# Twelve more projections of a hybrid attention/mLSTM layer computed in the seven-product stage, and what runs between the attention heads instead

## The chip, the cores and the metric

The kernel runs on one core of one Trainium2 chip. A core has a matrix engine (TensorE, "PE" in the profile; its weight loads are "PEld"), a vector engine (VectorE, DVE), an activation engine (ScalarE, ACT), GpSimd (POOL), SyncE (SP), which issues most transfers, and 16 DMA engines. The metric is the device time of one execution in microseconds (us). Three executions of the kernel before took 1817.91, 1818.23 and 1819.29 us; the median is 1818.23 us.

## The reference

One layer of a diffusion trunk for 640 tokens (128 context, 512 latent) of 1024 channels: a half-step SwiGLU feed-forward, then attention and an mLSTM (a chunkwise recurrent matrix memory) side by side on the same normalised input, then a second feed-forward. Cut to what matters here, with `h` the normalised input (640 x 1024):

```
mq, mk, mv, mo, mg, dq, dk, dv, gm, gd = split_cols(h @ p['w_in'][l])
dq = rmsnorm(dq, p['g_qn'][l]); dk = rmsnorm(dk, p['g_kn'][l])
q_att = rope_2d(dq)                                   # latent tokens
keys = jnp.concatenate([rope_2d(dk), k_ctx], axis=1)  # and the values with v_ctx
att = diff_attention(q_att, keys, vals, lam)          # 8 heads, 2 x 64 wide

# in it, for each block of 128 queries:
s = jnp.einsum('bqhcd,bkhcd->bhcqk', qi, kf) * scale
pr = jax.nn.softmax(s, axis=-1)
w = pr[:, :, 0] - lam * pr[:, :, 1]
out = jnp.einsum('bhqk,bkhv->bqhv', w, vf)

q = heads(mq) * (ML_HEAD_DIM ** -0.5)                 # 4 heads of 256: a factor of 1/16
h_f, st_f = mlstm_chunkwise(q, k, v, ...)             # k = heads(mk), v = heads(mv); and backwards
hm = rmsnorm(h_f + rev(h_b)) * jax.nn.sigmoid(mo)
y = jax.nn.sigmoid(gm) * (hm @ p['w_br_m'][l]) + jax.nn.sigmoid(gd) * (att @ p['w_br_d'][l])
```

The change is about where and how `mq`, `mk` and `mo` are computed. Everything is in float32; a product is made of three matmuls of split halves (high by high, high by low, low by high).

## The kernel before

The core keeps `h` transposed as two tiles `hH` and `hL` (high and low half; 8 blocks of 128 channels by 640 tokens). A weight slice of 1024 x 256, a *granule*, arrives as `raw` (1 MB) and is split into `wH` (by ACT) and `wL` (by DVE).

Three ways to project a granule occur:
- a **feature unit** (`feat_unit`, PSUM tile `ps_p`, four to a granule): 128 output channels by 320 tokens, 24 matmuls that each stream 320 columns;
- a **token unit** (`tok_unit`, `ps_t`, five to a granule): 128 tokens by 256 output channels, 24 matmuls of 256 columns;
- the **seven-product stage** (class `Winograd`, here its subclass `Gates`, `ps_f`): the granule is treated as a 2 x 2 block matrix, and seven products of 12 matmuls of 320 columns take the place of the eight that four feature units are. It needs sums of weight blocks (`ww`, `wB`, `wC`, made by DVE and ACT from `raw`) and sums of the four blocks of `h` (`S`, made once). Partial results `u` are added to others on DVE to `g_out`, which SP stores to DRAM.

The program in order: first feed-forward (to about 455 us of the span); the first pair's `q` and `k` as token units; `Gates`, six granules (`w_gd` and `w_gm`, three each; about 504 to 578 us); attention (to about 1065 us); the mLSTM loop, called the memory stage below (to about 1212 us); gates, output projection and second feed-forward.

Attention is eight heads (`hd`) of five query blocks (`qi`; blocks 0 to 3 against 768 keys, block 4 against 128). The loop at L1942 writes for each block: `scores` (PE, tile `sc`, then DVE's minimum `mn`), `turn` of the block before (PE transposes the weights `p` into `ps_wT`, ACT copies them to `wT`), `soft` (two exponentials on ACT), `mix` (DVE: `rc`, `r`, then `p`), `values` of the block before (PE: `ps_o` from `wT`; DVE: `ao`). At block 3 it writes `pack` of the next head (ACT: `qpk`, twice `kpk`; DVE: `qpk`), and at the head's end `queries` and `keys` (PE transposes them, ACT and DVE copy). Blocks under `with written()` keep the written order on each engine.

Between these steps PE gets units from a queue, `Fill` (L1244): `fill.units(n)` issues the next n units of the queue in its order, filled at L1757 to L1781. The table `UNITS` says how many go to the two places of each block and to the places at the head's end. The units of the attention's own later pairs (`project_q`, `project_k`, `project_v` of pairs 1 to 3) are in the same queue; after a pair's five units `qk_norm_rope` (L1467) normalises and rotates the tokens: ACT squares (`rope`), DVE sums (`ss`), multiplies by `ry` and the weight, ACT swaps halves (`rope`), DVE multiplies with two tables and adds. I call this a *rope* below. What is left in the queue after attention is issued in the memory stage.

`Columns` (L787) computes parts of the modulation vector: DVE multiplies and sums slices `raw_a` of a weight matrix, two instructions of 128 x 1024 to a tile. The memory stage holds twelve such tiles.

ACT and DVE take their instructions one after the other in the order of the program.

Of the kernel before, what the change touches and what calls it, by code (L numbers as in the profile page):

```python
# [16 lines left out]
D = 1024  # L17
# [14 lines left out]
def tile_trunk(ctx: ExitStack, tc: tile.TileContext, a: dict):  # L32
# [287 lines left out]
    class Winograd:  # L320
# [57 lines left out]
        def copy_of(self, p, tag, bufs=1):  # L378
            t = self.tmp.tile([128, HALF], F32, tag=tag, name="u", bufs=bufs)
            self.copied = act(t, p, AF.Copy)  # L380
            return t

        def products(self, work, between, then=(), ahead=None, prepared=False, narrow=0):
# [16 lines left out]
            for i, (gr, A, done, used) in enumerate(work):  # L400
# [32 lines left out]
                u2 = copy_of(Y, "nacc" if i < 2 * FB - 2 else "nsq", 2)  # L433
# [6 lines left out]
                u3 = copy_of(Y, "nry")  # L440
# [889 lines left out]
    gd_dram = dp.tile([128, KT, T], F32, name="gd_dram")  # L1330
    qq_dram = dp.tile([128, 2, T], F32, name="qq_dram")
# [130 lines left out]
    def rope_place(of):  # L1462
        if not in_pools:
            return rope_p[0].tile([128, 5, 256], F32, tag="pk", name="rope", bufs=2)
        return pair(of, 2, "rope").rearrange("p a b -> p (a b)").rearrange("p (t n) -> p t n", t=5)
# [39 lines left out]
    def project_k(pr, now=lambda f: f()):  # L1505
        def make():
            if pr % 2:
                t = pair("k", 3, "k_tok").rearrange("p a b -> p (a b)").rearrange("p (t n) -> p t n", t=5)
            else:
                t = qk.tile([128, 5, 256], F32, tag="ktok", name="k_tok")  # L1510
# [15 lines left out]
    def project_v(pr):  # L1526
        def make():
            v_tok[pr] = t = ap.tile([128, 7, 256], F32, tag="vtok", name="v_tok")
# [163 lines left out]
    def begin_pools():  # L1692
        gates.close()
        in_pools["k"] = ctx.enter_context(tc.tile_pool(name="mlk", bufs=1, side="right"))
        in_pools["q"] = queries_of.enter_context(tc.tile_pool(name="mlq", bufs=1, side="right"))
# [21 lines left out]
    def k_evac(h, by_act=False):  # L1717
        mkT[h] = pair("k", h, "mkT")
        if by_act:
            return lambda p, mt, hf: act(mkT[h][:, mt, half(hf)], p, AF.Copy)  # L1720
        return lambda p, mt, hf: vec.tensor_copy(mkT[h][:, mt, half(hf)], p)
# [18 lines left out]
    def queries_of_memory(h):  # L1740
        feature(a["w_mq"][h], lambda: q_evac(h))

    def keys_of_memory(h, **kw):
        feature(a["w_mk"][h], lambda: k_evac(h, **kw))

    def open_gate(h, pool):
        feature(a["w_mo"][h], lambda: o_evac(h, pool()))

# [17 lines left out]
    keys_of_memory(1)  # L1766
    values_of(1)
    token(project_v(2))
    values_of(2)
    projections(3)  # L1770
    open_gate(1, attention)
    values_of(3)
    token(project_v(3))
    queries_of_memory(2)
    keys_of_memory(2)
    queries_of_memory(3)
    keys_of_memory(3, by_act=True)
    open_gate(2, memory)
    open_gate(3, memory)
# [13 lines left out]
    class Gates(Winograd):  # L1793


        def __init__(self, fp, tmp, psum):
            self.fp, self.tmp, self.psum = fp, tmp, psum
            self.part = {(kh, hf): Of(kh, hf) for kh in range(2) for hf in range(2)}
            self.work = [
                [Granule(4, lambda raw, src=src[g]: dma(raw, src)), lambda i: self.ops[i], self.done(dst, g), lambda i: None]  # L1800
                for g in range(3) for src, dst in ((a["w_gd"], gd_dram), (a["w_gm"], gm_dram))
            ]
# [4 lines left out]
        def done(self, dst, g):  # L1807
            def f(mt, hf, p, u):
                t = self.tmp.tile([128, HALF], F32, tag=("nsq", "nt")[mt], name="g_out", bufs=2)
                if u is None:  # L1810
                    act(t, p, AF.Copy)
                else:
                    tt(vec, t, p, u, ALU.add)
# [73 lines left out]
    def between(i, at):  # L1887
        if at and i < 4:
            with tc.issue_after(G.work[i + 1][0].split_at):
                (lambda: None, tables, *ropes)[i]()  # L1890
        elif (i, at) == (len(G.work) - 2, 0):
# [3 lines left out]

    G.products(G.work, between, narrow=2)
    wide.close()
    early.close()
# [18 lines left out]
    def aside(hd, qi, part):  # L1917
# [11 lines left out]
    two, one = (1, 1), (1, 0)  # L1929
    UNITS = {  # L1930
        0: (two, two, two, two, two, (1, 1, 1)), 1: (two, two, two, one, one, (1,)),
        2: (two, two, two, two, two, (1, 1, 1)), 3: (two, two, two, one, one, (1,)),
        4: (two, two, two, two, two, (1, 1, 1)), 5: (two, two, two, two, one, (1,)),
        6: (one,) * 5 + ((0, 0, 0),), 7: (one,) * 4 + ((0, 0),),
    }
    late = None
    for hd in range(8):
        H = heads[hd]
        odd = hd % 2
        for qi in range(5):  # L1940
# [20 lines left out]
            if (hd, qi) == (0, 2):  # L1961
                begin_pools()
            fill.units(n[1])
# [5 lines left out]
        if hd < 7:  # L1969
# [6 lines left out]
            if odd:  # L1976
                for i in range(5):
                    fill.one()
                    if i in (0, 1):
                        N.keys(i)  # L1980
                    if i == 1:
                        with written():
                            fill.ahead()
            else:
# [555 lines left out]
```

## Time and profile before

| | |
|---|---|
| times | 1817.91, 1818.23, 1819.29 us |
| profiled execution | span 1816.4 us; its last instruction ends there, and the fastest of the three times lies 1.5 us above it, the median 1.8 us |
| PE busy | 1793.6 us (99%) |
| DVE busy | 1323.8 us (73%) |
| ACT busy | 894.8 us (49%) |
| POOL busy | 37.1 us (2%) |
| mean DMA rate | 169 GB/s |

"Busy" is the time in which an engine has an instruction under way. The PE's instruction ends are modelled and overlap, so what a matmul costs is read from the distance between starts of neighbours, not from its listed duration. A group's row names line, engine, operation, output and inputs, shapes and count, then total and mean time; after the bar follow the engine's idle time just before these instructions and what ended it. In a timeline row the first number is the start, the second the duration, and the bracket the idle time before. The shares of busy time are means over stages that have different limits.

### The profile page before, as it was taken

How to read it: one execution, taken by the hardware profiler on the slowest of the kernel's cores; microseconds unless marked ns; L12 is line 12 of the kernel's file. 1: busy time of each engine (PE TensorE's matmuls, PEld its weight loads, DVE VectorE, ACT ScalarE, POOL GpSimd, SP SyncE). 2: the span in 40 equal slices, each digit the busy share in tenths (PEclk: the TensorE clock that was granted, in tenths of full speed). 3: DMA queues.
4: the chain of work that ended last, by engine and by line, in shares of the span. 5: the costliest groups of instructions: out<-in, count | busy, mean ns of one | idle time of the engine just before them, and what ended most of it. 6: DMA issues, size and time to landing. Idle time of an engine off the chain costs nothing.

```text
span 1816.4 us, 30813 instructions
## 1 busy us (share of the span) xinstructions
PE 1793.6 (99%) x12622; PEld 1754.8 (97%) x12622; DVE 1323.8 (73%) x2140; ACT 894.8 (49%) x1558; POOL 37.1 (2%) x65
## 2 busy tenths in 40 slices
PE   9999999999999999999999999999999999999998
PEld 7999999999999999999999889999999999999998
DVE  6889986677886776475575649876767888897485
ACT  5654553333755454455465454674336545554432
POOL 0000000100000000000000000000000000000010
PEclk9999999999999999999999999999999999999999
DMA  8255566977244322112222055665652355657992
GB/s 330 106 197 183 185 224 235 344 228 257 82 138 159 106 76 78 63 63 89 80 89 72 20 169 163 223 254 183 238 170 80 134 172 185 202 181 275 352 307 83
DMA packets 130622, 307.69 MB, mean 169 GB/s; under 512 B 9841, under 2 KB 92017, under 8 KB 117553
## 3 DMA queue, kind: packets, MB, share of 16 engines
q1 hardware_dynamic: 120114, 263.64, 42.1%
q0 software_dynamic: 9680, 39.46, 6.7%
q8 instruction: 99, 1.62, 0.4%
q10 hardware_dynamic: 688, 2.63, 0.4%
q14 instruction: 41, 0.34, 0.1%
HBM read 238.14 MB, written 67.56 MB: 168 GB/s over the span
## 4 chain that ended last, share of the span: by engine, by line
PE 84%; DVE 7%; DMA 5%; ACT 3%; issue 1%; SPq 0%; DVEq 0%; ACTq 0%
PE ps_f L75 43%; PE ps_p L75 19%; PE ps_t L75 11%; PE sc L75 3%; PE ps_o L75 2%; DVE ww L54 2%; PE ps_n L75 2%; DMA raw<-in_w2b 2%; DMA raw_a<-in_w_ada_k 1%; PE ps_wT L78 1%; PE ps_u L75 1%; DVE junk L813 1%; PE ps_qkT L78 1%; DMA out_new_c<-Cn 1%; DMA P<-nm_dram 1%
## 5 line engine op out<-in xcount | busy, mean ns | idle before, releaser
L75 PE MATMUL ps_f<-S,ww 128*128 128x320 f32 x2184 | 352.5, 310 | 3.0 <-DMA S<-g_dram 1.0
L75 PEld LDWEIGHTS ps_f<-S,ww 128*128 128x128 f32 x2184 | 327.5, 188 | 7.0 <-DVE ww L54 4.6
L75 PE MATMUL ps_p<-hH,wH 128*128 128x320 f32 x672 | 212.4, 316 | 0.7 <-DVE stage L61 0.7
L75 PE MATMUL ps_p<-hH,wL 128*128 128x320 f32 x672 | 207.7, 309 | 0.0
L75 PE MATMUL ps_p<-hL,wH 128*128 128x320 f32 x672 | 207.7, 309 | 0.0
L54 DVE TENSOR_TENSOR ww<-raw,ww 128x2048 fp32r<-128x2048 f32 (+1 forms) x67 | 150.2, 2241 | 63.7 <-ACT ww L51 63.6
L75 PE MATMUL ps_f<-hm,ww 128*128 128x320 f32 x1176 | 185.8, 309 | 0.6 <-DVE ww L54 0.6
L75 PE MATMUL ps_t<-wH,hH 128*128 128x256 f32 x640 | 185.2, 289 | 0.9 <-DVE x L57 0.9
L75 PE MATMUL ps_t<-wH,hL 128*128 128x256 f32 x640 | 181.0, 283 | 0.9 <-DVE hL L54 0.9
L75 PE MATMUL ps_t<-wL,hH 128*128 128x256 f32 x640 | 180.8, 283 | 0.0
L75 PEld LDWEIGHTS ps_f<-hm,ww 128*128 128x128 f32 x1176 | 175.7, 188 | 1.2 <-DVE ww L54 1.2
L75 PE MATMUL ps_f<-hm,wB 128*128 128x320 f32 x1008 | 161.5, 309 | 0.0
L51 ACT ACTIVATE ww<-raw 128x2048 fp32r<-128x2048 f32 (+1 forms) x67 | 125.3, 1871 | 57.9 <-DVE raw L54 33.6
L75 PEld LDWEIGHTS ps_f<-hm,wB 128*128 128x128 f32 x1008 | 151.3, 188 | 0.0
L54 DVE TENSOR_TENSOR raw<-raw 128x1024 f32<-128x1024 f32 x168 | 145.3, 865 | 1.9
L75 PEld LDWEIGHTS ps_p<-hH,wH 128*128 128x128 f32 x672 | 126.4, 188 | 1.2 <-DVE stage L61 0.9
L75 PEld LDWEIGHTS ps_p<-hL,wH 128*128 128x128 f32 x672 | 126.3, 188 | 0.3
L75 PEld LDWEIGHTS ps_p<-hH,wL 128*128 128x128 f32 x672 | 126.2, 188 | 0.0
L51 ACT ACTIVATE u<-ps_f 128x320 f32<-128x320 f32 x117 | 50.7, 433 | 153.2 <-PE ps_f L75 153.1
L75 PEld LDWEIGHTS ps_t<-wH,hH 128*128 128x128 f32 x640 | 122.3, 191 | 1.5 <-ACT nsq L51 1.1
L75 PEld LDWEIGHTS ps_t<-wH,hL 128*128 128x128 f32 x640 | 122.3, 191 | 1.1 <-DVE hL L54 1.1
L75 PEld LDWEIGHTS ps_t<-wL,hH 128*128 128x128 f32 x640 | 122.5, 191 | 0.4
(307 smaller groups left out, 3444.8 us busy)
## 6 DMA issues: line engine op xcount, KB each, us to landing
g_dram<-g SPq DMA_DIRECT2D x44, 640.0 KB, 7.5
raw_a<-in_w_ada_c POOLq DMA_DIRECT2D x31, 512.0 KB, 4.7
g_dram<-g SPq DMA_DIRECT2D x24, 480.0 KB, 8.2
raw<-in_w1b SPq DMA_DIRECT2D x11, 1024.0 KB, 4.8
raw<-in_w3b SPq DMA_DIRECT2D x11, 1024.0 KB, 6.3
raw<-in_w1a SPq DMA_DIRECT2D x10, 1024.0 KB, 4.9
raw<-in_w3a SPq DMA_DIRECT2D x10, 1024.0 KB, 6.5
hm<-g_dram SPq DMA_DIRECT2D x7, 1280.0 KB, 13.3
```

Source lines behind the costliest of these rows:

```text
L51: return placed(nc.scalar.activation(*args, **kw))
L54: return placed(eng.tensor_tensor(out=out, in0=in0, in1=in1, op=op))
L75: tc.keep_in_program_order(nc.tensor.matmul(*args, **kw))
L78: tc.keep_in_program_order(nc.tensor.transpose(*args, **kw))
L813: placed(vec.tensor_tensor_reduce(out=junk, in0=raw, in1=self.csil[:, v, :], op0=ALU.mult, op1=ALU.add, scale=1.0, scalar=0.0, accum_out=m ...
```

## The change

The twelve granules `w_mq`, `w_mk`, `w_mo` (four heads each) leave the queue and join `Gates.work`, which has 18 granules instead of six. Their results go to DRAM (`mq_dram`, `mk_dram`, `o_dram`; the first two are new); keys are loaded again during head 6 (`load_keys`), queries after attention (`load_queries`). The queue holds token units only, except for the last two granules, and its order is heads' own projections first (`k`, `q`, `v` of pairs 1, 2, 3), then the memory's values. `UNITS` is one unit to a block and three at a head's end. Eight of the memory stage's twelve `Columns` tiles move into eight of the new granules. `q_tok` and `k_tok` of odd pairs, and every second `v_tok`, get a second place.

```diff
         def products(self, work, between, then=(), ahead=None, prepared=False, narrow=0):
...
-                u2 = copy_of(Y, "nacc" if i < 2 * FB - 2 else "nsq", 2)
+                scaled = getattr(gr, "scaled", {})
+                u2 = copy_of(Y, "nacc" if i < 2 * FB - 2 else "nsq", 2, **scaled)
...
-                u3 = copy_of(Y, "nry")
+                u3 = copy_of(Y, "nry", **scaled)
...
     def rope_place(of):
...
-        return pair(of, 2, "rope")...
+        return pair("k", "qk".index(of), "rope")...
...
-            q_tok[pr] = t = qk.tile([128, 5, 256], F32, tag="qtok", name="q_tok")
+            q_tok[pr] = t = (ap if pr % 2 else qk).tile([128, 5, 256], F32, tag="qtok", name="q_tok")
...
-    def o_evac(h, pool):
-        def f(p, mt, hf):
-            t = pool.tile([128, HALF], F32, tag="stage", name="stage", bufs=2)
-            ts(t, p, -43.0, ALU.max)
-            act(t, t, AF.Exp, scale=-1.0)
-            nc.sync.dma_start(out=o_dram[:, 2 * h + mt, half(hf)], in_=t)
-        return f
...
-    def q_evac(h):
+    def load_queries(h):
         mqT[h] = pair("q", h, "mqT")
-        return lambda p, mt, hf: act(mqT[h][:, mt, half(hf)], p, AF.Copy, scale=0.0625)
+        nc.sync.dma_start(out=mqT[h], in_=mq_dram[:, 2 * h : 2 * h + 2, :])
...
     token(project_v(0))
-    open_gate(0, attention)
     values_of(0)
-    projections(1)
-    queries_of_memory(0)
-    keys_of_memory(0)
-    token(project_v(1))
-    queries_of_memory(1)
-    projections(2)
...
-    open_gate(3, memory)
+    for pr in range(1, 4):
+        projections(pr)
+        token(project_v(pr))
+    for h in range(1, 4):
+        values_of(h)
     gate_unit(a["w_gm"], gm_dram, 3, memory)
     gate_unit(a["w_gd"], gd_dram, 3, memory)
...
+            gate = [(a[n], dst, g, self.plain) for g in range(3) for n, dst in (("w_gd", gd_dram), ("w_gm", gm_dram))]
+            qk = [(a[n], dst, h, f) for h in range(4) for n, dst, f in (("w_mq", mq_dram, self.query), ("w_mk", mk_dram, self.plain))]
+            o = [(a["w_mo"], o_dram, h, self.opening) for h in range(4)]
+            self.work = []
+            for src, dst, g, f in gate[:5] + qk[:3] + o[:1] + qk[3:5] + o[1:2] + qk[5:7] + o[2:3] + qk[7:] + o[3:] + gate[5:]:
+                gr = Granule(4, lambda raw, src=src[g]: dma(raw, src))
...
+        elif (i, at) in IN_GATES:
+            columns.tile(G.at_vec)
...
+    IN_GATES = [(i, 1) for i in (5, 6, 7, 9, 10, 12, 13, 15)]
...
-    two, one = (1, 1), (1, 0)
-    UNITS = {
-        0: (two, two, two, two, two, (1, 1, 1)), 1: (two, two, two, one, one, (1,)),
-        2: (two, two, two, two, two, (1, 1, 1)), 3: (two, two, two, one, one, (1,)),
-        4: (two, two, two, two, two, (1, 1, 1)), 5: (two, two, two, two, one, (1,)),
-        6: (one,) * 5 + ((0, 0, 0),), 7: (one,) * 4 + ((0, 0),),
-    }
+    one = (1, 0)
+    UNITS = {hd: (one,) * 5 + ((1, 1, 1),) for hd in range(7)}
+    UNITS[5] = UNITS[6] = (one,) * 5 + ((1, 1, 0),)
+    UNITS[7] = (one,) * 4 + ((0, 0), (0, 0))
...
+            elif hd == 6 and qi < 4:
+                load_keys(qi)
...
-            fill.drain(5)
+            fill.drain(2)
...
+    load_queries(0)
...
-    fill.pace(1.4, 1)
+    fill.pace(0.6, 1)
...
-    columns.place(12, csil2, load_columns_raw, 1)
+    for h in range(1, 4):
+        load_queries(h)
+    columns.place(4, csil2, load_columns_raw, 1)
...
-            if n in ((3, 5, 7, 8), (1, 3, 6, 8), (1, 3, 5, 7), ())[h]:
+            if n in ((5,), (3, 7), (5,), ())[h]:
                 columns.tile(m.at_vec)
```

How this moves instructions is shown at three places. The first is DVE in head 1, from the minimum of block 3 (the reduction of its scores `sc`) to block 4's `p`. Before:

```order
L1614 TENSOR_REDUCE mn_7940<-sc_7931 128x2
L54 TENSOR_TENSOR wL_7927<-raw_7738,wH_7926 128x2048
L1628 RECIPROCAL rc_7942<-sm_7941 128x2
L57 SCALAR_TENSOR_TENSOR r_7986<-sm_7941,nlam_5309,rc_7942 128x1
L57 SCALAR_TENSOR_TENSOR p0_7955<-p1_7956,r_7986,p0_7955 128x768
L61 TENSOR_SCALAR ao_7412<-ps_o_7990,rc_7844 128x128
L54 TENSOR_TENSOR qpk_7998<-q_tok_6819,qpk_7998 128x5x128
L1614 TENSOR_REDUCE mn_8035<-sc_8030 128x2
L54 TENSOR_TENSOR kL_8150<-ck_8171,kH_8149 128x2x256
L1628 RECIPROCAL rc_8037<-sm_8036 128x2
L57 SCALAR_TENSOR_TENSOR r_8080<-sm_8036,nlam_5309,rc_8037 128x1
L57 SCALAR_TENSOR_TENSOR p0_8050<-p1_8051,r_8080,p0_8050 128x128
```

After, from block 2's `ao`, which stands right behind block 3's `p`, to block 4's minimum:

```order
L61 TENSOR_SCALAR ao_8135<-ps_o_8612,rc_8451 128x128
L54 TENSOR_TENSOR kL_8694<-ck_8715,kH_8693 128x2x256
L57 SCALAR_TENSOR_TENSOR rt_8509<-ry_8508 128x20
L54 TENSOR_TENSOR rt_8509<-rt_8509,rv_8507 128x20
L57 SCALAR_TENSOR_TENSOR ry_8508<-rt_8509,ry_8508 128x20
L54 TENSOR_TENSOR q_tok_8239<-q_tok_8239,ry_8508 128x1280
L54 TENSOR_TENSOR q_tok_8239<-q_tok_8239,g_qn_5295 128x256
L54 TENSOR_TENSOR rope_8517<-rope_8517,ropeBq_5314 128x1024
L54 TENSOR_TENSOR q_tok_8239<-q_tok_8239,ropeAq_5313 128x1024
L54 TENSOR_TENSOR q_tok_8239<-q_tok_8239,rope_8517 128x1024
L54 TENSOR_TENSOR qpk_8620<-q_tok_8239,qpk_8620 128x5x128
L1614 TENSOR_REDUCE mn_8631<-sc_8626 128x2
```

Before, the second pair's query rope was over by then, and one subtraction (`qpk`) stood between block 3's `p` and block 4's minimum. After, the rope's second half stands there, because the fifth unit of `q_tok_8239` is issued in block 2 of this head.

The second place is ACT at the same point, from the second exponential of block 3 (`p1`) on. Before:

```order
L51 ACTIVATE p1_7956,sm_7941<-sc_7931,mn_7940 128x768
L51 ACTIVATE qpk_7998<-q_tok_6819 128x5x2x64
L51 ACTIVATE kpk_8001<-k_tok_6542 128x10x64 x2
L51 ACTIVATE k_tok_7899<-ps_t_7960 128x256
L51 ACTIVATE k_tok_7899<-ps_t_8004 128x256
L51 ACTIVATE kH_8149<-ck_8171 128x2x256
L51 ACTIVATE wT_8039<-ps_wT_8040 128x512
L51 ACTIVATE wT_8039<-ps_wT_8046 128x256
L51 ACTIVATE p0_8050,sm_8036<-sc_8030,mn_8035 128x128
```

After:

```order
L51 ACTIVATE p1_8567,sm_8552<-sc_8542,mn_8551 128x768
L51 ACTIVATE v_tok_8580<-ps_t_8582 128x256
L51 ACTIVATE kH_8693<-ck_8715 128x2x256
L51 ACTIVATE rt_8509<-rv_8507 128x20
L51 ACTIVATE ry_8508<-rt_8509 128x20
L51 ACTIVATE rope_8517<-q_tok_8239 128x1024
L51 ACTIVATE v_tok_8580<-ps_t_8650 128x256
L51 ACTIVATE qpk_8620<-q_tok_8239 128x5x2x64
L51 ACTIVATE kpk_8623<-k_tok_7846 128x10x64 x2
L51 ACTIVATE wT_8635<-ps_wT_8636 128x512
L51 ACTIVATE wT_8635<-ps_wT_8642 128x256
L51 ACTIVATE p0_8646,sm_8632<-sc_8626,mn_8631 128x128
```

Before, `qpk` follows the exponentials at once, as `q_tok_6819` is ready; the copies `wT_8039` of block 3's weights come behind the packing. After, `qpk_8620` needs the rotated `q_tok_8239`, and the copies `wT_8635` of block 3's weights still stand behind it.

The third place is SP's queue where the memory stage begins (`P` is a decay matrix, `va` the values, `C` the state, `csil` the conditioning vector). Before:

```order
L97 DMA mask_11300<-in_mask 128x256
L97 DMA P_11302<-nm_dram_4640 128x5x128 x2
L97 DMA va_11303<-v_dram_4635 128x5x256
L97 DMA C_11313<-in_c_aug 128x516
L97 DMA C_11315<-in_c_aug 128x516
L97 DMA csil_11317<-csil_dram_88 128x2048
L2023 DMA P_11456<-nm_dram_4640 128x5x128 x2
L2026 DMA va_11457<-v_dram_4635 128x5x256
```

After:

```order
L1705 DMA mqT_11798<-mq_dram_4639 128x1280
L97 DMA mask_11809<-in_mask 128x256
L97 DMA P_11811<-nm_dram_4642 128x5x128 x2
L97 DMA va_11812<-v_dram_4635 128x5x256
L97 DMA C_11822<-in_c_aug 128x516
L97 DMA C_11824<-in_c_aug 128x516
L97 DMA csil_11826<-csil_dram_88 128x2048
L1705 DMA mqT_11828<-mq_dram_4639 128x1280
L1705 DMA mqT_11830<-mq_dram_4639 128x1280
L1705 DMA mqT_11832<-mq_dram_4639 128x1280
```

One load of queries (128 x 1280, 640 KB) stands ahead of the first `P`, and three behind `csil`.

More of the change, by code (lines that the diff above doesn't have):

```diff
@@ L1506, in make @@
         def make():
[L1507 to L1510, printed above, removed]
+            t = (ap if pr % 2 else qk).tile([128, 5, 256], F32, tag="ktok", name="k_tok")
             k_tok[pr] = t
@@ L1527, in make @@
         def make():
-            v_tok[pr] = t = ap.tile([128, 7, 256], F32, tag="vtok", name="v_tok")
+            v_tok[pr] = t = ap.tile([128, 7, 256], F32, tag="vtok", name="v_tok", bufs=2)
             nc.sync.dma_start(out=t[:, 4:6, :], in_=a["cache_v"][:, :, pr * 256 : (pr + 1) * 256])
@@ L1975, in tile_trunk @@
             H.finish_norm()
[L1976 to L1984, printed above, removed]
-                N.keys(0)
-                fill.units(n[1])
-                N.keys(1)
-                with written():
-                    fill.ahead()
-                fill.units(n[2])
+            N.keys(0)
+            fill.units(n[1])
+            N.keys(1)
+            with written():
+                fill.ahead()
+            fill.units(n[2])
             late = H.finish
@@ L2000, in tile_trunk @@
     att.close()
+    in_pools["q"] = queries_of.enter_context(tc.tile_pool(name="mlq", bufs=1, side="right", reuse_waits="tile"))
+    load_queries(0)
     ml = ExitStack()
```

76 lines of the change are left out of this document (38 added, 38 removed).

## The prediction

> **What bounds the kernel now.** I read the page first: busy shares, clock and the chain that ended last.
>
> ```profile
> PE 1793.6 (99%) x12622; PEld 1754.8 (97%) x12622; DVE 1323.8 (73%) x2140; ACT 894.8 (49%) x1558; POOL 37.1 (2%) x65
> PEclk9999999999999999999999999999999999999999
> PE 84%; DVE 7%; DMA 5%; ACT 3%; issue 1%; SPq 0%; DVEq 0%; ACTq 0%
> ```
>
> PE is busy in 99% of the span at the full granted clock, and 84% of the chain lies on it. So a matmul that goes saves its whole time, unless PE then waits. The stretches by stage say what cover each stage has: the seven-product stage, attention, memory, and two pieces of the last.
>
> ```profile
> 504.00:578.00 74.00, 74.00 (x507) 74.00 (x506) 55.84 (x77) 37.72 (x57) 0.00 (x0) 1.00 0.46 156
> 578.00:1065.00 487.00, 482.96 (x3796) 473.52 (x3796) 294.93 (x452) 250.13 (x509) 0.00 (x0) 1.00 0.23 79
> 1065.00:1212.00 147.00, 144.11 (x848) 131.66 (x847) 123.29 (x360) 91.61 (x232) 0.00 (x0) 1.00 0.60 198
> 1080.00:1100.00 20.00, 20.00 (x124) 18.52 (x123) 18.85 (x56) 11.12 (x31) 0.00 (x0) 1.00 0.29 87
> 1060.00:1080.00 20.00, 17.73 (x106) 15.73 (x106) 9.45 (x23) 12.25 (x36) 0.00 (x0) 1.00 0.79 263
> ```
>
> The columns are the stretch, its length, the busy time of PE, PEld, DVE, ACT and POOL with counts, the clock, the DMA share and GB/s. PE idles for nothing in the seven products, 4 us in attention and 3 us in memory. Attention's DVE is busy for 295 of 487 us, memory's for 123 of 147.
>
> **The saving.** A stretch of the timeline prices PE's work by distances between starts; these rows stand between a feature unit and the next block of attention.
>
> ```profile
> 750.79 0.31 PE L75 MATMUL ps_p<-hH,wH 128*128 128x320 f32 x1
> ...
> 753.29 0.31 PE L75 MATMUL ps_p<-hH,wL 128*128 128x320 f32 x1
> ...
> 753.44 1.50 PE L75 MATMUL ps_o<-v_tok,wT 128*128 128x128 f32 x12
> ...
> 754.69 0.36 PE L75 MATMUL ps_t<-wH,hH 128*128 128x256 f32 x1
> ...
> 757.64 0.40 PE L75 MATMUL sc<-kH,qT 128*128 128x512 f32 x1
> ...
> 759.04 0.82 PE L78 MATMUL ps_wT<-ident,p 128*128 128x128 f32 x6
> ...
> 759.61 0.36 PE L75 MATMUL ps_t<-wH,hH 128*128 128x256 f32 x1
> ```
>
> The first two rows are 17 matmuls apart: 2.50/17 = 0.147 us each. The stage of the seven products has the same price, 74.00/507 = 0.146. Four feature units are 96 matmuls (14.1 us), seven products 84 (12.3 us). Twelve granules save 12 x 12 x 0.147 = **21.1 us** of PE.
>
> **What they meet in the seven products.** DVE's 55.84 us over six granules, the first pair's two ropes included, are at most 9.3 us per granule. Eight granules also take a `Columns` tile from the memory stage:
>
> ```profile
> L813 DVE CUSTOM_DVE_ANT_0 raw_a<-raw_a,csil 128x1024 bf16<-128x1024 f32 x24 | 29.1, 1212 | 0.0
> PEld ps_f L75 <- DVE ww L54: 5.8, 14, 0.8
> ```
>
> Two such instructions are 2.4 us, so DVE has at most 11.7 of 12.3 us, ACT some 8; the PE work of the granule hides them. Bounds: nothing, as in this stage before, or the mean wait for `ww` in all such stages, 5.8/14 = 0.41 us, in each of twelve granules, 5 us. The stage's own row is nearest; I take **+1**. The new stores and loads of `raw` are at the rate of the present stage, whose DMA share is 0.46.
>
> **What attention loses.** Before, blocks had two units as long as ropes were in progress. Now each has one, and the rows above make a block `ps_o` 1.25, unit 2.95, scores 1.40, transposes 0.57: 6.2 us of PE. Head 6 of before has such blocks already:
>
> ```profile
> 973.24 1.76 DVE L1614 TENSOR_REDUCE mn<-sc 128x2 f32<-128x1536 f32 x1 [0.26 <-PE sc L75]
> ...
> 979.63 1.76 DVE L1614 TENSOR_REDUCE mn<-sc 128x2 f32<-128x1536 f32 x1 [0.78 <-PE sc L75]
> ...
> 983.79 1.02 DVE L57 SCALAR_TENSOR_TENSOR p<-p,r,p 128x768 f32<-128x768 f32 x1
> ...
> 985.89 1.76 DVE L1614 TENSOR_REDUCE mn<-sc 128x2 f32<-128x1536 f32 x1 [0.82 <-PE sc L75]
> ```
>
> Minima start 6.39 and 6.26 us apart, and DVE waits 0.8 us for the scores: a block without a rope holds, with under a microsecond to spare. The minimum's start to `p`'s end is 5.2 us. A rope does not fit into that. Its pieces, from the groups of attention by shape:
>
> ```profile
> L54 DVE TENSOR_TENSOR wL<-raw,wH 128x2048 fp32r<-128x2048 f32 x24 | 54.9, 2286 | 18.4 <-ACT wH L51 18.3
> L1472 DVE TENSOR_REDUCE ss<-rope 128x20 f32<-128x1280 f32 x6 | 8.9, 1478 | 0.0
> L54 DVE TENSOR_TENSOR q_tok<-q_tok,ry 128x1280 f32<-128x1280 f32 x3 | 4.5, 1491 | 0.1
> L54 DVE TENSOR_TENSOR q_tok<-q_tok,g_qn 128x256 f32<-128x256 f32 x3 | 1.3, 419 | 0.0
> L54 DVE TENSOR_TENSOR rope<-rope,ropeBq 128x1024 f32<-128x1024 f32 x3 | 3.7, 1217 | 0.0
> L54 DVE TENSOR_TENSOR q_tok<-q_tok,ropeAq 128x1024 f32<-128x1024 f32 x3 | 3.7, 1219 | 0.0
> L54 DVE TENSOR_TENSOR q_tok<-q_tok,rope 128x1024 f32<-128x1024 f32 x3 | 3.6, 1208 | 0.0
> L54 DVE TENSOR_TENSOR kL<-ck,kH 128x512 fp32r<-128x512 f32 x8 | 5.5, 686 | 0.2
> ```
>
> ```profile
> L51 ACT ACTIVATE wT<-ps_wT 128x512 f32<-128x512 f32 x32 | 19.1, 598 | 26.3 <-PE ps_wT L78 26.2
> L51 ACT ACTIVATE kpk<-k_tok 128x640 fp32r<-128x640 f32 x14 | 9.5, 731 | 0.0
> L51 ACT ACTIVATE qpk<-q_tok 128x640 fp32r<-128x640 f32 x7 | 5.1, 735 | 0.7 <-DVE q_tok L54 0.7
> L51 ACT ACTIVATE rope<-q_tok 128x1024 f32<-128x1024 f32 x3 | 3.2, 1058 | 5.9 <-DVE q_tok L54 5.9
> ```
>
> *Head 1, block 3*, from its minimum's start. DVE: 1.76, then `wL` 2.29 and `ss` 1.48 give 5.53; `rc`, `r`, `p` end at 7.0 (5.2 without). Behind it `ao` 0.35, `kL` 0.69, three small ones 0.5, `ry` 1.49, `g_qn` 0.42: 10.45. ACT swaps (1.06): 11.5. Two products and the sum (1.22, 1.22, 1.21): 15.15. Only now can ACT do `qpk` (0.73) and `kpk` twice (1.46), and behind these the first `wT` copy of block 3 (0.60): 17.9. PE in the same time has transposes 0.57, a unit 2.95, `ps_o` 1.25, block 4's short scores about 0.5 (estimated from two of the eight matmuls), block 3's transposes and a second unit: it reaches those transposes at 5.3, is held for `p` until 7.0, and stands at block 3's `ps_o` from 10.5 to 17.9. That is 1.7 + 7.4; block 4's `p`, behind the minimum and two exponentials, costs about 0.9 more: **10 us**. Waiting behind ACT's `qpk` are `wT` and the exponentials, behind DVE's `qpk` the minimum; all of PE's next work waits for these.
>
> *Head 3, block 3.* `ry` and `g_qn` stand ahead of `p` (end 5.6), and `ropeBq`, `ropeAq`, `kL`, the sum behind it: with `ao` 10.3. `qpk`, `kpk`, `wT`: 13.1. PE is at `ps_o` at 8.8 + 0.3 = 9.1: 4.0, and 1 at block 4: **5 us**.
>
> *The other four ropes* (into heads 1, 3, 5, and head 5's query) lie where a head's end has three units or where parts are spread over blocks; their sums exceed the 6.2 us or the end's work by 1 to 3 us each, estimated from the same durations: **6 us**. Together +21. Below, the trace's nearest evidence is the block of head 6 whose 2.29 us `wL` caused no wait, by which about 6 us would be left; above, 28, if each of the four also holds a copy behind `qpk`.
>
> The ends of heads 6 and 7 get a unit or two that they lacked; there 1000 to 1065 us shows 1.7 us of idle PE:
>
> ```profile
> 1000.00:1065.00 65.00, 63.29 (x442) 61.19 (x443) 31.28 (x54) 27.36 (x57) 0.00 (x0) 1.00 0.18 60
> ```
>
> I take **-1** (-1.7 to 0).
>
> **What memory loses.** Ten feature units leave, 35.2 us of PE (already in the saving): 144.1 to 108.9. DVE loses eight tiles, 8/12 of 29.1 and of their accumulator reads (2), and 3.9 of the output gates: 123.3 to about 98.7. DVE then has 91% of PE's work, and single heads have more than PE. Added up instruction by instruction from the durations of this stage's groups, in the changed order, the four heads have 22.0, 28.4, 28.2 and 28.7 us of DVE against 21.7, 26.3, 29.8 and 26.4 of PE: 0.3 + 2.1 + 2.3 uncovered. I take **+5**. The bounds: 0, as the row of 1080 to 1100 hides 94% fully, and 10, twice the sum, if waits of single steps come on top.
>
> **Seams.** Queries of 640 KB each stand on SP ahead of and behind the first `P`:
>
> ```profile
> DVE P L54 <- DMA P<-nm_dram: 7.6, 4, 2.6
> ```
>
> DVE already waits 7.6 us there in four times, with 0.79 of the DMA busy at 1060 to 1080. One or two such waits may reach PE, likewise the gate loads at attention's start, behind the stage's last stores: **+3** (0 to 8, all four waits).
>
> **Sum.** -21.1 + 1 + 21 - 1 + 5 + 3 = +7.9, so a span of 1824.3. The median of the runs lies 1.8 us above the profiled span: **1826.1 us**. The bounds add up to -16.8 and +29.9: 1801 and 1848.
>
> **The rivals.**
> - *The ropes hide, and the kernel is faster.* DVE waits in attention for PE's scores in most blocks; if its rope pieces start earlier than my sums have them, PE waits only where `qpk` holds the copies. Decisive is whether the ropes and memory together cost under 17 us. For it: DVE's 192 idle us in attention, and `wL` in head 6 without a wait. Against it: an idle microsecond ahead of a block doesn't help a chain that starts with the fifth unit. With ropes 10, memory 2, seams 1: 1818.2 - 21.1 + 1 + 10 - 1 + 2 + 1 = 1810 (1804 to 1815).
> - *Memory becomes DVE's.* DVE sets the pace head by head (10), and all seams land (8): 1826 + 5 + 5 = 1836. For it the 123 of 147 us; against it the stretch at 94%.
> - *The clock falls behind the long waits.* The granted clock is 1.00 throughout, and PE's waits are short; the longest of the first row of the list of waits is 1.4 us:
>
> ```profile
> PE ps_a L75 <- DMA raw_a<-in_w_ada_k: 2.8, 2, 1.4
> ```
>
> Waits of 7.4 and 4.0 us would be new. If the block after each ran at half the rate, it would cost 6.2 us more: up to 1838, about 1832. The Trainium skill says in "TensorE: Matmul & The Clock Gate", Part 1: The HAM clock gate, that PE's clock halves after an idle window of some 3.4 us and returns after a busy one; by that, an estimate is 1.7 us for each wait, 1829.5. No run here shows it yet.
> - *The price doesn't hold:* a granule of the longer stage takes as long as four feature units, since DVE's 11.7 of 12.3 us slip. Then the saving is gone: 1847. Six granules without idle PE speak against it.
>
> **How the numbers follow.** A measurement of this kernel can tell about 0.2%, 3.6 us, from no change: the same is 1814.6 to 1821.9. The forecast, ropes that hold PE at some 20 us, has 0.51, of it 0.11 in that band and 0.40 slower. Hidden ropes have 0.28 (0.25 faster, 0.03 same). Memory has 0.10, the clock 0.07, the price 0.04, all slower. That makes 0.25 faster, 0.14 the same, 0.61 slower. The range leaves out the last rival and the edges of the first two: 1806 to 1840. The forecast's own range is 1816 to 1836.
>
> **What would show it.** After the change the seven-product stage must last 18 x 12.3 = 222 us with PE full. In head 1, ACT's `wT` behind `qpk` must wait for DVE, and PE idle before `ps_o` for about 7 us once, in head 3 for about 4. Memory should last near 113 us. If PE shows no gap of over 2 us in attention, the ropes are the step that failed; if the granted clock leaves 1.00 there, the third rival holds; if the stage has gaps at `ww`, the fourth.

## The result: 1846.67 us, slower by 1.5%

The changed kernel takes 1846.67 us (median of four runs, 1844.63 to 1847.47) against 1818.76 us before: a ratio of 1.0149, 95% interval 1.0137 to 1.0161. That is 27.9 us more, where 7.9 were forecast, and outside the range (1806 to 1840). Its profiled execution has a span of 1845.5 us. The page after, in the lines for busy time and for the chain:

```profile
PE 1789.0 (97%) x12478; PEld 1742.9 (94%) x12478; DVE 1379.7 (75%) x2212; ACT 924.9 (50%) x1614; POOL 41.4 (2%) x73
PE 79%; DVE 9%; DMA 5%; ACT 5%; issue 1%; SPq 0%; DVEq 0%; ACTq 0%
```

The saving is there: 12622 - 12478 = 144 matmuls fewer, 144 x 0.147 = 21.1 us. But PE's share of the span and of the chain falls, and DVE and ACT now stand in the chain. The stages of the kernel after, as stretches: the seven products, attention, memory up to its last state update, and memory's tail up to the last head's last `ps_hT` (columns as in the prediction).

```profile
506.10:728.10 222.00, 222.00 (x1515) 222.00 (x1515) 169.42 (x222) 106.49 (x161) 4.22 (x8) 1.00 0.50 169
728.10:1119.90 391.80, 366.40 (x2933) 352.00 (x2932) 266.68 (x423) 222.34 (x475) 0.00 (x0) 0.98 0.24 78
1119.90:1241.00 121.10, 111.83 (x607) 97.93 (x606) 94.23 (x314) 79.22 (x213) 0.00 (x0) 0.97 0.55 176
1241.00:1267.60 26.60, 20.83 (x131) 20.50 (x131) 12.46 (x31) 20.59 (x34) 0.00 (x0) 0.87 0.66 252
```

The seven products are what was forecast: 222 us and no idle PE. Attention has 25 us of idle PE (4 before), memory 9 (3 before), the tail 6; and the granted clock is below 1.00 in three of the four, which it was in none of these stages before. The list of PE's waits names the steps:

```profile
PE ps_o L75 <- ACT wT L51: 10.7, 4, 6.3
PE ps_hT L78 <- DVE hs L57: 9.8, 2, 5.8
PE ps_wT L78 <- DVE p L57: 6.5, 8, 1.3
PE sc L75 <- ACT p L51: 6.0, 9, 1.8
```

Busy time counts a matmul at half rate as busy. So I also add up, over PE's instructions, how far the next start lies beyond the median distance for that kind in the trace of before; I call it *lost* PE time. Stage length and lost time for all kernels below (us, from the start times):

```
               seven prod.   attention     memory        tail
before          74.2   0     487.1  14.7   146.9   6.5   25.8  0.5
after          222.1   0     391.8  44.5   121.1  14.3   26.6  8.2
e1_order       222.1   0     383.3  36.4   120.3  13.6   26.5  8.2
e2_norope      222.1   0     368.1  21.6   120.3  13.5   27.4  9.1
e3_columns     222.1   0     390.4  43.1   112.6   6.1   27.2  8.9
e4_fillers     197.4   0     394.4  46.9   136.6   6.2   22.3  0.5
e5_tail        209.7   0     393.0  46.1   121.1   4.3   35.7 13.9
e6_order2      222.1   0     381.3  34.7   120.8  14.1   26.5  8.1
e7_joint       209.7   0     384.0  37.2   121.3   4.5   36.5 14.6
e8_pace        222.1   0     389.8  43.0   115.5  15.8   25.8  0.5
e9_joint2      222.1   0     381.3  34.6   104.3   4.6   25.8  0.5
e10_first      222.0   0     385.1  38.5   104.0   4.4   25.8  0.5
e11_pool       222.1   0     399.0  51.5   105.2   5.6   25.8  0.5
e12_shift      222.1   0     391.0  44.7   105.0   5.4   25.8  0.5
e13_cover      185.1   0     405.0  16.9   109.2   9.5   25.8  0.5
```

From before to after the lost time in these stages grows from 21.7 to 67.0: 45 us against 21 saved. The stretch up to the seven products, whose code is the same, took 502.9 us in the one trace and 505.0 in the other, and 502.7 to 507.3 in the others: some 2 us of the difference are that. In the trace of the kernel after, matmuls run at half rate for 3.4 us of it, near 36 us, which lost 1.9 us; in that of before they do not.

### The profile page after: what moved, and what is told of

Read it like the earlier page. It is cut to its first block, busy times and chain, and to the rows that moved or that the text cites. A ratio compares the mean times of both kernels' runs of the same rounds, so it can differ in the third digit from the quotient of the medians.

```text
span 1845.5 us, 30801 instructions
## 1 busy us (share of the span) xinstructions
PE 1789.0 (97%) x12478; PEld 1742.9 (94%) x12478; DVE 1379.7 (75%) x2212; ACT 924.9 (50%) x1614; POOL 41.4 (2%) x73
## 4 chain that ended last, share of the span: by engine, by line
PE 79%; DVE 9%; DMA 5%; ACT 5%; issue 1%; SPq 0%; DVEq 0%; ACTq 0%
PE ps_f L75 52%; PE ps_p L75 9%; PE ps_t L75 8%; PE sc L75 2%; PE ps_o L75 2%; DVE ww L54 2%; DMA raw_a<-in_w_ada_k 1%; PE ps_n L75 1%; PE ps_wT L78 1%; DVE mn L1614 1%; ACT p L51 1%; DVE wL L54 1%; DMA raw<-in_w2b 1%; DVE junk L814 1%; PE ps_qkT L78 1%
## 5 line engine op out<-in xcount | busy, mean ns | idle before, releaser
L75 PE MATMUL ps_f<-S,ww 128*128 128x320 f32 x2616 | 421.8, 310 | 2.8 <-DMA S<-g_dram 0.9
L75 PEld LDWEIGHTS ps_f<-S,ww 128*128 128x128 f32 x2616 | 392.3, 188 | 6.7 <-DVE ww L54 4.6
L54 DVE TENSOR_TENSOR ww<-raw,ww 128x2048 fp32r<-128x2048 f32 (+1 forms) x79 | 177.7, 2249 | 82.0 <-ACT ww L51 81.7
L54 DVE TENSOR_TENSOR raw<-raw 128x512 f32<-128x512 f32 (+1 forms) x204 | 176.6, 866 | 2.7
L54 DVE TENSOR_TENSOR wB<-raw,wB 128x1024 fp32r<-128x1024 f32 x70 | 85.4, 1220 | 22.5 <-ACT wB L51 22.5
L814 DVE CUSTOM_DVE_ANT_0 junk<-raw_a,csil 128x1024 bf16<-128x1024 f32 (+1 forms) x78 | 95.1, 1219 | 6.8 <-DMA raw_a<-in_w_ada_c 6.5
L51 ACT ACTIVATE wB<-raw 128x1024 fp32r<-128x1024 f32 x70 | 73.6, 1052 | 39.2 <-PE ps_f L75 17.0
L75 PE MATMUL ps_p<-hH,wH 128*128 128x320 f32 x288 | 90.0, 312 | 1.5 <-DVE C L57 1.5
L75 PE MATMUL ps_p<-hH,wL 128*128 128x320 f32 x288 | 89.2, 310 | 0.0
L75 PE MATMUL ps_p<-hL,wH 128*128 128x320 f32 x288 | 89.1, 310 | 0.0
```

The lines of the kernel that those rows point to most:

```text
L51: return placed(nc.scalar.activation(*args, **kw))
L54: return placed(eng.tensor_tensor(out=out, in0=in0, in1=in1, op=op))
L75: tc.keep_in_program_order(nc.tensor.matmul(*args, **kw))
L814: placed(vec.tensor_tensor_reduce(out=junk, in0=raw, in1=self.csil[:, v, :], op0=ALU.mult, op1=ALU.add, scale=1.0, scalar=0.0, accum_out=m ...
```

## Experiments

**The first wait: a rope ahead of the packing.** This is the timeline of the kernel after in head 1, from block 3's `p` to PE's next work (DVE, ACT and PE rows in order of time).

```profile
828.80 1.02 DVE L57 SCALAR_TENSOR_TENSOR p<-p,r,p 128x768 f32<-128x768 f32 x1
...
831.24 1.49 DVE L54 TENSOR_TENSOR q_tok<-q_tok,ry 128x1280 f32<-128x1280 f32 x1
...
836.25 1.22 DVE L54 TENSOR_TENSOR q_tok<-q_tok,rope 128x1024 f32<-128x1024 f32 x1
```

```profile
837.51 0.74 ACT L51 ACTIVATE qpk<-q_tok 128x640 fp32r<-128x640 f32 x1 [3.40 <-DVE q_tok L54]
838.15 1.35 ACT L51 ACTIVATE kpk<-k_tok 128x640 fp32r<-128x640 f32 x2
839.40 0.85 ACT L51 ACTIVATE wT<-ps_wT 128x512 f32<-128x512 f32 x2
```

```profile
829.97 0.85 PE L78 MATMUL ps_wT<-ident,p 128*128 128x128 f32 x6 [1.24 <-DVE p L57]
840.03 2.29 PE L75 MATMUL ps_o<-v_tok,wT 128*128 128x128 f32 x9 [6.35 <-ACT wT L51]
...
930.61 2.93 PE L75 MATMUL ps_o<-v_tok,wT 128*128 128x128 f32 x12 [3.02 <-ACT wT L51]
```

It is the chain of the prediction, step by step: 1.2 and 6.4 us where 1.7 and 7.4 were summed. The last row is the same place in head 3: 3.0 us (4.0 summed). Whether the rope's place or its work matters was tested in three ways.

*e1_order* moves the memory's first values behind the second pair's queries:

```diff
     token(project_v(0))
-    values_of(0)
     for pr in range(1, 4):
         projections(pr)
+        if pr == 1:
+            values_of(0)
         token(project_v(pr))
```

> The memory's first values (five units) go behind the second pair's queries, so that the second pair's query rope falls into the end of head 0 and the start of head 1 instead of block 3 of head 1. Theory A (a rope that stands ahead of the packing holds PE, and long waits cost clock): the 6.5 us wait ahead of ps_o in head 1 and the half-rate stretch behind it go, 1846.7 minus 9 to 13: about 1836. Rival R (blocks with one unit lack cover wherever the rope lies, its 10 us of VectorE are lost at any place): within 3 us of 1846.7, with the idle time spread over other blocks.

Measured: 1839.6 us (1838.6 to 1842.4), 7 us less. The 6.4 us wait is gone, and head 1's lost time falls from 13.5 to 3.7 us; head 0 takes 1.9 of it, so that the gain is below the 9 to 13 expected.

*e2_norope* leaves out norm and rotation of the queries and keys of pairs 1 to 3, by a return at the head of `qk_norm_rope` once attention has begun.

> Norm and rotation of the queries and keys of pairs 1 to 3 are left out (the output is not the reference's), all else stays in place. Theory A: of attention's 44 us of idle or slowed PE about 25 to 29 go: about 1819. Rival R (the chain minimum, exponentials, mix is too long for a block with one unit, rope or not): at most 10 us go, 1837 or more. If it lies between, the ropes are only part.

Measured: 1822.9 us. Attention's stretch:

```profile
725.80:1093.90 368.10, 360.22 (x2933) 348.07 (x2932) 225.51 (x363) 207.66 (x454) 0.00 (x0) 1.00 0.25 83
```

Attention is 391.8 - 368.1 = 23.7 us shorter with the same matmuls (x2933): that is what the ropes cost, for 266.7 - 225.5 = 41 us of DVE. Still, 21.6 us of lost time stay, more than the 14.7 that attention had before with its ropes; of the surplus, 3.3 us lie in head 0.

*e6_order2* changes only the order of the queue; all of the memory's values go behind attention's own projections (`values_of(h)` for h from 0 to 3 behind the loop over pairs).

> Only the order of the queue: the memory's four value granules all go behind attention's own projections, so that every later rope starts five units earlier and falls at a head's end or just behind it. Theory A (place of the rope, not its work): of the 23 us that the ropes cost, 6 to 9 are left: 1846.7 minus 15: about 1832. Rival R (VectorE and ScalarE have no room for a rope at any place): no better than e1_order, 1839.

Measured: 1836.7 us (1835.8 to 1841.9), 10 less, not 15. Attention loses 34.7 us; by e2_norope 13 of these are ropes. This place for the ropes gets back nearly half of their cost; no third order of the queue was tried.

**The second wait: memory.** PE waits twice for `hs`, the normalised result of a head. The first time (timeline, DVE and PE rows of the kernel after):

```profile
1160.62 1.21 DVE L814 CUSTOM_DVE_ANT_0 raw_a<-raw_a,csil 128x1024 bf16<-128x1024 f32 x1
...
1162.89 1.22 DVE L814 CUSTOM_DVE_ANT_0 raw_a<-raw_a,csil 128x1024 bf16<-128x1024 f32 x1
...
1164.15 2.06 DVE L57 SCALAR_TENSOR_TENSOR hs<-hs,ry,g_mh 128x256 f32<-128x256 f32 x5
```

```profile
1164.69 0.69 PE L78 MATMUL ps_hT<-ident,hs 128*128 128x128 f32 x2 [4.08 <-DVE hs L57]
```

A column tile's two instructions stand among the last steps of the statistics, ahead of `hs`. DVE is busy for only 94 of the stage's 121 us, so its load alone does not explain the wait; whether the place does was tested.

*e3_columns* computes all twelve tiles in the seven products:

```diff
-    IN_GATES = [(i, 1) for i in (5, 6, 7, 9, 10, 12, 13, 15)]
+    IN_GATES = [(i, 1) for i in range(5, 17)]
...
-    columns.place(4, csil2, load_columns_raw, 1)
...
-            if n in ((5,), (3, 7), (5,), ())[h]:
-                columns.tile(m.at_vec)
```

> All twelve column tiles are computed in the twelve new granules of the seven products, none in the memory stage. Theory C (a column tile ahead of the finishing of a head on VectorE holds ps_hT in memory): the 4.3 us wait before ps_hT and the slow stretch behind it go, 5 to 8 us: about 1840; the seven products stay at 222 us unless VectorE, near 12 of 12.3 us in granules with an output gate, falls behind. Rival F (the memory stage lacks matmuls of its queue to put beside its chains): within 2 us of 1846.7, the wait moves to another step.

Measured: 1838.8 us (1837.0 to 1845.2), 8 less; the first wait for `hs` falls to 0.7 us, memory is 8.4 us shorter, at the lost time of before (6.1 against 6.5), and the seven products stay at 222.1 us.

*e4_fillers* takes the output gates of heads 2 and 3 out of `Gates.work` and back into the queue (as before the change), with `fill.drain(4)` and `fill.pace(1.2, 1)`.

> Two output gates (heads 2 and 3) go back from the seven products to the queue, as feature units in the memory stage. That adds 3.5 us of PE. Rival F: memory's 22 us of idle or slowed PE fall to about 10, net 1838. Theory C: the waits stay, since they stand behind VectorE and a weight load: 1847 to 1850.

Measured: 1833.7 us (1831.0 to 1834.9), 13 less. Theory C said that the waits would stay; both went. So both hold: the tile in the chain makes the wait, and a matmul from the queue beside it hides it.

The second time is the tail. ACT's timeline in the kernel after, and PE's row:

```profile
1244.73 1.91 ACT L51 ACTIVATE wH<-raw 128x2048 fp32r<-128x2048 f32 x1 [1.99 <-DMA raw<-in_w_brd]
1246.55 0.40 ACT L51 ACTIVATE hjunk<-hs 128x256 f32<-128x256 f32 x1
```

```profile
1250.71 0.69 PE L78 MATMUL ps_hT<-ident,hs 128*128 128x128 f32 x2 [5.77 <-DVE hs L57]
```

The split of a branch weight, which waits for its transfer, stands ahead of three of the last head's five sums of squares (`hjunk`).

*e5_tail* is e3_columns with one output gate (head 3) back in the queue, `fill.drain(3)` and a pace of 0.9.

> As e3_columns (all column tiles in the seven products), and one output gate (head 3) goes back to the queue, so that four feature units more lie in the memory stage. Theory A (memory's remaining loss is its tail: ScalarE waits for a branch weight ahead of the last head's statistics because the queue runs dry early): the 5.6 us wait before ps_hT goes, 1838.8 minus 8 plus 1.8 for the dearer granule: about 1832. Rival (the tail waits for the transfer however much stands before it): 1838 to 1841, wait still there.

Measured: 1846.4 us. Both were wrong: the wait grew to 11.6 us. *e7_joint* joined it with e6_order2.

> e5_tail and e6_order2 together. If the causes add: 1846.7 - 15 (ropes) - 8 (columns) - 6 (tail) = 1818, no different from the kernel before at 1818. If a gap that goes in one place only moves to another: 1826 or more.

Measured: 1835.7 us, with the same tail. There ACT takes a gate's sigmoid (`sig`) between the steps of the statistics, with a load of its function table (`ACT_TABLE_LOAD`) at each change:

```profile
1231.91 1.28 ACT L51 ACT_TABLE_LOAD   x1
1233.20 0.21 ACT L51 ACTIVATE rt<-rv 128x5 f32<-128x5 f32 x1
1233.43 1.28 ACT L51 ACT_TABLE_LOAD   x1
1234.72 1.27 ACT L51 ACTIVATE sig<-sig 128x1280 f32<-128x1280 f32 x1
1236.01 1.28 ACT L51 ACT_TABLE_LOAD   x1
1237.30 0.21 ACT L51 ACTIVATE ry<-rt 128x5 f32<-128x5 f32 x1
```

So the order on ACT in the tail turns on how many units are left there. *e8_pace* is the kernel after with `fill.pace(0.45, 1)`:

> The change with one number altered: the pace of the queue in the memory stage is 0.45 instead of 0.6, so that two of its eight units are left for the end of the stage, and ScalarE's statistics of the last head then stand ahead of the second branch weight instead of behind it. Theory A (memory's tail is ScalarE's order: statistics behind a weight split that waits for its transfer): the 5.8 us wait before the last head's ps_hT and the slow stretch behind it go, 1846.7 minus 6 to 8: 1840. Rival (too little work left at the tail, whatever the order): the wait stays or shrinks by under 2 us, 1845 or more; and the two units taken from the stage's middle cost up to 3.

Measured: 1838.6 us (1835.4 to 1840.0), 8 less. All five sums now stand ahead of the split:

```profile
1235.14 0.42 ACT L51 ACTIVATE hjunk<-hs 128x256 f32<-128x256 f32 x1
...
1242.49 1.90 ACT L51 ACTIVATE wH<-raw 128x2048 fp32r<-128x2048 f32 x1
```

The tail loses 0.5 us, with two units (7 us of PE) more in it; memory and tail are 6.4 us shorter together. But the run changes two things, the order on ACT and the work beside it. This is where `hs` starts in the kernel after, and then in e8_pace:

```profile
1250.17 2.07 DVE L57 SCALAR_TENSOR_TENSOR hs<-hs,ry,g_mh 128x256 f32<-128x256 f32 x5
```

```profile
1240.31 2.07 DVE L57 SCALAR_TENSOR_TENSOR hs<-hs,ry,g_mh 128x256 f32<-128x256 f32 x5
```

The last matmul of the state update (`ps_u`) starts at 1241.05 and at 1232.82. So `hs` comes 9.1 us behind it in the kernel after and 7.5 us in e8_pace: the better order brought 1.6 us. From the same point PE has work for 3.9 us in the kernel after and for 10.9 us in e8_pace. By these numbers the two units alone would have covered the wait, and the order alone would have left some 4 us of it (5.8 less 1.6); neither was run alone. A bad order can be worse than units can cover: in e5_tail, with 7.4 us of work, `hs` comes after 18.4 us.

**The three together.** *e9_joint2* joins e6_order2, e3_columns and e8_pace.

> The queue's order of e6_order2, the columns of e3_columns and the pace of e8_pace together, all twelve granules in the seven products. If the three causes add: 1846.7 - 10 - 8 - 7 = 1822, still 3 above the kernel before: what is left are the ropes that fall into one-unit blocks (13 of 23 us) and the gate rows in head 0. If not: 1828 or more.

Measured: 1820.1 us (eleven runs, 1818.2 to 1822.0), ratio to before 1.0004 (0.9995 to 1.0013): no difference. The causes add: 10 + 8 + 8 = 26, and 1846.7 - 1820.1 = 26.6. Memory then loses 4.6 us; what keeps the 21 us of saving from showing is attention's 34.6.

*e10_first* gives head 0 two units in its first two blocks (`UNITS[0] = ((1, 1), (1, 1), one, one, one, (1, 1, 1))`).

> As e9_joint2, with two units in the first two blocks of head 0, where VectorE and ScalarE compute the memory's gate rows. Theory A: head 0's 5.8 us of idle or slowed PE fall to about 3, and the ropes of heads 1 to 5 shift by two units: 1820. Rival: nothing gained, since the two units are missing behind attention (where they cover memory's first loads): 1822 to 1824.

Measured: 1820.8 us (1819.5 to 1829.9). The time is the one that Theory A gave, 1820, but the account is the rival's. In the trace, whose execution took 1825.0 us and so lies 4 above the median, heads 0 to 6 lose 23.4 us instead of 29.9, but head 7 and what follows it up to memory 14.8 instead of 4.4. Its longest wait of PE, 4.3 us, is there, where the two units are missing:

```profile
PE ps_aT L78 <- DVE ao L54: 5.7, 2, 4.3
```

Nothing is gained.

*e11_pool* is e9_joint2 with `wL` on GpSimd during the heads.

> As e9_joint2, with the low halves wL of the twelve weight granules that are split between the heads computed on GpSimd instead of VectorE: 12 x 2.29 = 27 us of VectorE less in attention. If what is left of the ropes' cost is VectorE's load, 5 to 8 us of attention's 35 us of idle or slowed PE go: 1820 minus 5 to 8, about 1814. Rival: GpSimd is slow or gets in VectorE's way (no run here shows its elementwise rate, and of GpSimd on two operands none is in the traces), so that wL comes late or VectorE's own instructions get longer: 1820 or slower.

Measured: 1836.7 us, 17 slower than e9_joint2. GpSimd's group, and one group of DVE in e9_joint2 and then in e11_pool:

```profile
L54 POOL TENSOR_TENSOR wL<-raw,wH 128x2048 fp32r<-128x2048 f32 x12 | 55.8, 4650 | 349.2 <-ACT wH L51 325.1 <-PE ps_qkT L78 24.1
```

```profile
L54 DVE TENSOR_TENSOR kL<-ck,kH 128x512 fp32r<-128x512 f32 x7 | 4.8, 683 | 0.0
```

```profile
L54 DVE TENSOR_TENSOR kL<-ck,kH 128x512 fp32r<-128x512 f32 x7 | 12.6, 1806 | 3.3 <-ACT kH L51 3.3
```

So the rival's side held: GpSimd needs 4.65 us for a `wL`, and VectorE's own instructions get longer. How much of the 17 us comes from each was not separated.

*e12_shift* moves one unit of the ends of heads 0 to 4 into an early block.

> As e9_joint2, with one unit of the ends of heads 0 to 4 moved into a block near the start of the head (block 1 of head 3, block 0 of the others), so that the number of units to a head is the same. Theory A (a block with two units, 9 us of PE, hides gate rows or a piece of a rope): heads 0, 1, 3 and 4 lose 21 us now and will lose 12 to 15; the ends, with two units as in heads 5 and 6, lose at most 0.5 each more: 1813 to 1816. Rival: the ends need their third unit: 1820.

Measured: 1827.5 us (1824.3 to 1829.5), 7 slower than e9_joint2. Heads 2 and 3 lose 8.4 and 7.1 us instead of 3.1 each, most of the difference in their first block. The largest sum in the list of PE's waits is now of this kind: two waits, in the first blocks of heads 3 and 4, where the head before is finished:

```profile
PE ps_aT L78 <- DVE ao L54: 7.3, 2, 3.7
```

The ends need their three units, as the rival said, though its 1820 missed as well: attention has no unit to spare. *e13_cover* therefore buys some. Three output gates (heads 0 to 2) leave the seven products again, and their twelve units become second units of early blocks; the twelve column tiles go into the nine granules that stay:

```diff
     def projections(pr):
         token(project_k(pr))
+        open_gate(pr - 1, attention)
         token(project_q(pr))
...
+    for hd, n in enumerate((4, 2, 2, 1, 2, 1)):
+        UNITS[hd] = ((1, 1),) * n + UNITS[hd][n:]
```

> As e9_joint2, with three output gates (heads 0 to 2) taken out of the seven products again: they are twelve feature units of the queue, put as second units into the first blocks of heads 0 to 5, where gate rows and ropes run. That costs 3 x 1.76 = 5.3 us of PE. Theory A (what attention still loses is cover in those blocks): its 35 us of idle or slowed PE fall to about 18, as before the change: 1820 + 5 - 16 = 1809, faster than both kernels. Rival (the ropes cost about the same with two units in a block, or shift to others): 1818 to 1825.

Measured: 1810.5 us (1809.0 to 1812.9), ratio to before 0.9958 (0.9944 to 0.9973): faster than both kernels. Attention:

```profile
691.30:1096.30 405.00, 399.03 (x3221) 388.58 (x3220) 275.37 (x437) 232.09 (x487) 0.00 (x0) 1.00 0.27 87
```

288 matmuls more (x3221 against x2933), 23.7 us longer than e9_joint2 instead of 288 x 0.147 = 42: the lost time falls from 34.6 to 16.9. The ropes move with the units: in this trace the last step of each of the six ropes starts in a block with two units, in e9_joint2 five of the six in a block with one. Memory loses 9.5 us instead of 4.6, so that the whole gains 9.6 us.

## Why the prediction was wrong

**The saving and the seven products** were right: 21.1 us of PE gone, 18 granules in 222 us. The +1 was 0.

**The ropes** were right in mechanism and place: PE waited before `ps_o` in heads 1 and 3 for 6.35 and 3.02 us, where about 7 and 4 were named. The size came out partly by luck. Forecast were +21, and 23.7 are measured by leaving the ropes out; but 4.0 of these are matmuls at half rate behind the two waits (2.4 and 1.6), which the sum left to a rival. In heads 1 and 3, forecast at 10 and 5, the lost time is 11.9 and 7.0 us above that without ropes (13.5 - 1.6 and 8.7 - 1.7), and 9.5 and 5.4 without the half rate.

**The rest of attention** was the step that failed first. The prediction took two quiet blocks of head 6 as proof that a block without a rope "holds", and put -1 (-1.7 to 0) on the remainder. Without any rope, attention loses 21.6 us against 14.7 before: +6.9. Most blocks without a rope do hold: they lose 0.2 us in e2_norope, as before. What was not priced is other work in blocks that have lost their second unit, first of all the memory's gate rows, which DVE and ACT compute in head 0: head 0 loses 4.6 us instead of 1.3, of it 3.6 in its first two blocks, and with two units there (e10_first) these lose 0.2. Heads 4 and 6 add 1.8 and 1.2 us; what holds PE there was not tried. That second units are what is missing, for ropes and the rest together, e13_cover shows: twelve of them get back 17.7 us.

**Memory** was the second: +5, and +3 for the seams, against 22.5 - 7.0 = 15.5; the stage lasted 121.1 us, not about 113. The working compared sums, DVE's microseconds with PE's, head by head, and the sums were near: 107.3 us of DVE for the four heads, and 106.7 measured in memory and tail. The loss came from two places in the order: a column tile ahead of `hs` (8.4 us by e3_columns), and in the tail a weight split ahead of the statistics with too little work of PE beside it (6.4 by e8_pace, which changed both). The seams, the loads of queries, cost nothing that can be seen: with the columns gone, memory lost what it lost before. The memory rival named the stage, but for DVE's load, and with 1836 stopped short.

**The clock rival** came true as well, as a part of these numbers. Five stretches at half rate in attention, memory and tail lost 1.6 to 2.4 us each, 10.0 together; the trace of before has none there. Behind the two waits that the rival named, 2.4 and 1.6 us were lost, where it had 6.2 for a whole block at half rate, and 1.7 as an estimate.

With the measured sizes the sum is -21.1 + 0 + 23.7 + 6.9 + 15.5 = 25.0, and 27.1 with the 2.1 us of the first stretch; 0.8 of the measured 27.9 stay open. Against the forecast the rest of attention is 7.9 too high, memory and seams 7.5, the ropes 2.7. The full bounds, 1801 to 1848, held the time; the range that was kept, to 1840, left no room for several terms that run high together. They did so for one reason in part: units put back take waits away in attention (e13_cover) and in memory (e4_fillers) alike.

## What to carry to other kernels

Matmuls that are taken from a stage may be its cover: before they go, list for each chain that they stand beside (packing, statistics, gates) what PE does meanwhile without them. Read the order of the in-order engines, not only their sums: an instruction that waits ahead of one that is needed costs as much on an idle engine as on a full one. Where cover is short, pay for a little of it at the blocks that need it: here three of twelve granules, 5.3 us of PE, brought back 17.7 us of lost time in attention.

## What the runs showed of the hardware

The clock. In head 1 the granted clock fell to 0.50 some 4.6 us into the wait, which began at 833.7, and stayed there until 845, into 5 us of work. But a wait of 1.8 us, which begins at 761.2 in head 0, was enough too (kernel after, PE's row and stretches of 1 us):

```profile
762.99 0.60 PE L75 MATMUL sc<-kH,qT 128*128 128x512 f32 x1 [1.78 <-ACT p L51]
```

```profile
762.00:763.00 1.00, 0.01 (x1) 0.02 (x1) 0.04 (x1) 1.00 (x4) 0.00 (x0) 1.00 1.19 218
763.00:764.00 1.00, 1.00 (x3) 0.80 (x4) 0.93 (x3) 1.00 (x2) 0.00 (x0) 0.62 0.60 45
764.00:765.00 1.00, 1.00 (x6) 1.00 (x5) 0.44 (x1) 1.00 (x1) 0.00 (x0) 0.50 0.79 58
```

In e9_joint2 the same wait was as long, and the clock stayed:

```profile
763.68 0.50 PE L75 MATMUL sc<-kH,qT 128*128 128x512 f32 x1 [1.75 <-ACT p L51]
```

```profile
762.00:763.00 1.00, 0.00 (x0) 0.00 (x0) 0.00 (x0) 1.00 (x3) 0.00 (x0) 1.00 0.84 328
763.00:764.00 1.00, 0.32 (x1) 0.30 (x2) 0.30 (x2) 1.00 (x4) 0.00 (x0) 1.00 0.27 10
764.00:765.00 1.00, 1.00 (x8) 0.85 (x6) 0.96 (x2) 1.00 (x1) 0.00 (x0) 1.00 0.97 69
```

The Trainium skill gives an idle window of some 3.4 us in "TensorE: Matmul & The Clock Gate", Part 1: The HAM clock gate, and calls the window free-running; the measurement differs in that a wait of 1.8 us can do, or not. The fifteen traces of this case (behind their first 60 us) show how far that goes. All 20 waits of PE of 3.59 us or more dropped the clock; of those from 1.75 to 3.55 us some did and some did not, and the wait of 3.0 us in head 3 dropped it in the kernel after, e3_columns and e4_fillers, but not in e1_order, e5_tail and e8_pace. Three drops have no wait as long near them, but two of 0.7 to 1.3 us close together (e2_norope, e12_shift, e13_cover). Behind the single waits the drop came 1.9 to 5.0 us after the wait began. Unless the trace ended first, each stretch at half rate lasted 3.4, 6.8, 10.2 or 13.7 us. In the kernel after, the five of them in attention, memory and tail cost 1.6 to 2.4 us each.

GpSimd takes 4.65 us for the 128 x 2048 subtraction that takes DVE 2.29, and while it runs, some of DVE's own two-operand instructions are held. Of the seven `kL` in e11_pool five took 0.68 us, as in e9_joint2, and the two that ran beside a `wL` on GpSimd 4.62 us each, nearly as long as that `wL`. One of the two (POOL's and DVE's rows):

```profile
1061.06 4.54 POOL L54 TENSOR_TENSOR wL<-raw,wH 128x2048 fp32r<-128x2048 f32 x1 [29.21 <-ACT wH L51]
```

```profile
1061.53 4.62 DVE L54 TENSOR_TENSOR kL<-ck,kH 128x512 fp32r<-128x512 f32 x1 [1.67 <-ACT kH L51]
```

How the two share was not tried further.
